# Rows of the normed activations at multiples of 256 bytes, and narrower stationary operands for one level of scores

## The chip, the cores and the metric

The kernel runs on one core of a Trainium2 chip. The metric is the device time of one execution in microseconds (us), the median of several runs. The profile shows one execution, instruction by instruction. TensorE appears there twice: PE for the products, PEld for the loads of the stationary operand. DVE is VectorE, ACT is ScalarE, POOL is GpSimd, SP issues the transfers from memory.

## The reference

One decoder layer over 16 meta tokens and 512 tokens of width 1024, in float32. Cut to what matters here:

```python
n = rmsnorm(h, norm_mix_g[l])                       # h: 16 meta tokens, then x
proj = n @ w_in[l]
zq, zf, zi, zog, zpool, zga, zgb = jnp.split(proj, SPLIT_POINTS, axis=-1)
...
o = hgrn2_chunked(...)                              # per head: decayed scores of q and k, times v
y_a = o * silu(zog);  y_b = pooled(zpool) @ pool_w * pool_scale
merged = sigmoid(zga) * (y_a @ w_branch_a[l]) + sigmoid(zgb) * (y_b @ w_branch_b[l])
h = h + merged @ w_out[l]
n2 = rmsnorm(h, norm_ffn_g[l])
h = h + (jax.nn.silu(n2 @ w_ffn_gate[l]) * (n2 @ w_ffn_up[l])) @ w_ffn_down[l]
return rmsnorm(h, norm_final_g)[:, N_META:]
```

## The kernel before

**Products in three terms.** Each large product is made in the type float32r from operands that are split into a high and a low part: high by high, low by high and high by low are added in one accumulator (`mm3`, lines 154 to 156). The weights stream from memory in blocks of 128 x 1024 (`wr`); ACT casts the high part (`wh`, line 130) and DVE subtracts for the low part (`wl`, line 137). In `product` a block of weights is the stationary operand, 128 columns at a time, and the transposed activations are the moving operand, 512 columns at a time, or in two pieces of 256 and 272 where the 16 meta tokens are needed too (`METAS`). In `token_major` (the output product `po` and the down product `pd`, lines 763 to 765) it is the other way round: the activations are stationary and 512 columns of weights move.

**The activations that move.** The first norm, transposed, lies in `nTh` and `nTl`: 128 partitions, 8 rows of `TT` = 528 elements each, one row for each 128 of the width (`k` in the code). A row is 528 x 4 = 2112 bytes, which is 8 times 256 and 64 more. So the rows begin at 0, 64, 128 and 192 bytes past a multiple of 256, and the same again for rows 4 to 7. They feed `pj_f`, `pj_v`, `pj_p` (pieces of 256 and 272) and `pj_q`, `pj_gb`, `pj_og`, `pj_ga` (512). The second norm lies in `n2h` and `n2l` with the same shape, in the same memory, though only 512 of the 528 columns are used; it feeds `pj_fg` and `pj_fu`, the gate and up products of the FFN. All other moving operands (`yah`, `ybh`, and the weights themselves in `po` and `pd`) have rows of 2048 or 1024 bytes and begin at multiples of 1024.

**Scores by levels.** The recurrence (`hgrn`, for four groups of two heads) computes its scores by levels of h = 1, 2, 4, ... 64. A level's products go into one bank `psc`; ACT copies the result into `scT`. Levels 16, 32 and 64 are made at line 523: for each 128-token block, keys of h tokens are stationary (h columns) and queries of the next h tokens move. These are float32 products, which the trace shows as two passes each. Level 64 has 8 products per group, 64 stationary by 64 moving columns.

**The order.** The program is written as generators that are woven together: after each step of `hgrn` some 6 to 9 steps of products for other branches follow (`weave`). A scheduler orders each engine's instructions from that.

Of the kernel before, what the change touches and what calls it, by code (L numbers as in the profile page):

```python
# [8 lines left out]
F32 = mybir.dt.float32  # L9
F32R = mybir.dt.float32r  # L10
# [5 lines left out]
P = 128  # L16
D = 1024
T = 512
NM = 16
TT = T + NM  # L20
KT = D // P
NH = 8
NG = 4
# [13 lines left out]
def hybrid_layer(ctx: ExitStack, tc: tile.TileContext, x, meta_tokens, norm_mix_g, w_in, lb_raw,  # L37
                 hgrn_norm_g, pool_w, pool_scale, w_branch_a, w_branch_b, w_out, norm_ffn_g,
                 w_ffn_gate, w_ffn_up, w_ffn_down, norm_final_g, out):
    nc = tc.nc  # L40
    cst = ctx.enter_context(tc.tile_pool(name="cst", bufs=1))
    wp = ctx.enter_context(tc.tile_pool(name="wp", bufs=3))
    big = ctx.enter_context(tc.tile_pool(name="big", bufs=1))
# [12 lines left out]
    def t5(name, cols=T):  # L56
        return sm.tile([P, TT], F32, tag="t5", name=name, bufs=8)[:, 0:cols]

    def bank(pool, name):
        return pool.tile([P, 512], F32, tag=pool.name, name=name)  # L60
# [134 lines left out]
        add_rows(w_ffn_down, DFF, half * 512, 512, 2)  # L195


    nTh = big.tile([P, KT, TT], F32R, tag="bigA", name="nTh")
    nTl = big.tile([P, KT, TT], F32R, tag="bigB", name="nTl")

    def squares(src, rows, name):
        sq = g4t(f"sq_{name}")
# [49 lines left out]
    nc.sync.dma_start(pw, pool_w[0].rearrange("g c d -> c g d"))  # L252


    par = cst.tile([P, 29], F32, name="par")
    lmx = cst.tile([P, 8], F32, name="lmx")
    le = cst.tile([P, 16], F32, name="le")
    lb = cst.tile([P, 8], F32, name="lb")
# [4 lines left out]
    def load_parameters():  # L263
        pps = bank(psm, "pps")
        nc.tensor.transpose(pps[:, 0:29], prow[0:29, :], ident[0:29, 0:29])
        nc.vector.tensor_copy(par, pps[:, 0:29])

    def parameters():
        nc.vector.tensor_tensor(lmx, par[:, 0:8], par[:, 8:16], ALU.max)
# [7 lines left out]

    NT = lambda k: (nTh[:, k, :], nTl[:, k, :])  # L280

    def pair(hs, ls):
        def f(k):
# [4 lines left out]
    def product(name, mov, nk, done, cuts=((0, T),)):  # L288

        pss = [[bank(psm, f"pj_{name}{j}{i}")[:, 0:b - a] for i, (a, b) in enumerate(cuts)] for j in range(2)]  # L290
        for k0 in range(0, nk, 4):
            wh, wl = W.get()
            for j in range(2):
                js = slice(j * P, (j + 1) * P)
                for k in range(4):
                    mh, ml = mov(k0 + k)
                    for ps, (a, b) in zip(pss[j], cuts):
                        mm3(ps, wh[:, k, js], wl[:, k, js], mh[:, a:b], ml[:, a:b],
                            k0 + k == 0, k0 + k == nk - 1)
                    yield  # L300
                if k0 + 4 == nk:
                    done(j, pss[j])

    CUT = 256
    METAS = ((0, CUT), (CUT, TT))

# [4 lines left out]
    def load_group(g, first=False):  # L311
# [7 lines left out]
        def f_done(hh, ps):  # L319
# [4 lines left out]
            nc.scalar.activation(fv[:, CUT:T], p1[:, 0:T - CUT], AF.Sigmoid)  # L324
            nc.scalar.activation(Fm[:, hh, :], p1[:, T - CUT:TT - CUT], AF.Sigmoid)
            for t, o in ((fv, kk[:, hh * T:(hh + 1) * T]), (Fm[:, hh, :], km[:, hh, :])):
# [7 lines left out]
        else:  # L334
            yield from product(f"f{g}", NT, KT, f_done, METAS)

        vT = []

        def v_done(hh, ps):
            t = t5(f"vT{g}{hh}", TT)  # L340
            nc.scalar.copy(out=t[:, 0:CUT], in_=ps[0])
            nc.scalar.copy(out=t[:, CUT:TT], in_=ps[1])
            vT.append(t)

        yield from product(f"v{g}", NT, KT, v_done, METAS)

# [4 lines left out]

        for i, _ in enumerate(product(f"q{g}", NT, KT, q_done)):
            yield
# [14 lines left out]
    def first_product(done):  # L368
# [13 lines left out]
        def part(i, b, passes=range(3)):  # L382
            a, e = METAS[i]
            h, l = W.parts[b]
            for p in passes:
                for j in range(2):
                    js = slice(j * P, (j + 1) * P)
                    for k in range(4):
                        mh, ml = NT(4 * b + k)
                        nc.tensor.matmul(pss[j][i], (h, l, h)[p][:, k, js], (mh, mh, ml)[p][:, a:e],  # L390
                                         start=b == 0 and p == 0 and k == 0, stop=b == 1 and p == 2 and k == 3)
# [31 lines left out]
        part(0, 1, (2,))  # L423
        mt = g4t("mt")[:, 0:KT * NM].rearrange("p (k t) -> p k t", t=NM)
        tm = bank(psh, "tp_m").rearrange("p (k t) -> p k t", t=NM)[:, 0:KT, :]
# [41 lines left out]
    def hgrn(g):  # L467

        F, kk, qq, Fm, km, vt, vm = grp[g]
        scT, Q, tt = g4t(f"scT{g}"), g4t(f"Q{g}"), g4t(f"tt{g}")  # L470
# [35 lines left out]
        for h in (1, 2, 4, 8, 16, 32, 64):  # L506
            ps = bank(psh, f"psc{g}_{h}")
            if h == 1:
                for c in range(4):
                    nc.tensor.matmul(ps[32 * c:32 * c + 32, 0:P], ones, E.rearrange(  # L510
                        "p (i w b) -> p i w b", i=8, w=4)[:, :, c, :], start=True, stop=True)
            elif h <= 8:
                n = 32 if h == 2 else 16
                for i, c in wins:
                    o = (4 * i + c) * 32
                    mv = M2[:, 4 * i + c, :] if h == 2 else halves(Q[:, o:o + 32], h)[1]
                    nc.tensor.matmul(ps[32 * c:32 * c + 32, i * n:(i + 1) * n], kk[:, o:o + 32], mv,
                                     start=True, stop=True)
            else:
                for i in range(8):  # L520
                    for b in range(0, P, 2 * h):
                        o = i * P + b
                        nc.tensor.matmul(ps[b:b + h, i * h:(i + 1) * h], kk[:, o:o + h],
                                         Q[:, o + h:o + 2 * h], start=True, stop=True)
            if h == 4:

                pk = bank(psh, f"pkm{g}")
                for hh in range(2):
                    nc.tensor.transpose(pk[:NM, hh * P:(hh + 1) * P], km[:, hh, :], ident)
                kmT = sm.tile([NM, 2 * P], F32, tag="kmT", name=f"kmT{g}", bufs=1)  # L530
                nc.vector.tensor_copy(kmT, pk[:NM, 0:2 * P])
            if h == 16:
                pS = bank(psh, f"pS{g}")
                for hh in range(2):
                    hs = slice(hh * P, (hh + 1) * P)
                    nc.tensor.matmul(pS[:, hs], kmT[:, hs], vm[:, hs], start=True, stop=True)
                S = sm.tile([P, 2 * P], F32, tag="S", name=f"S{g}_0", bufs=5)
                nc.vector.tensor_copy(S, pS[:, 0:2 * P])
                Ss = [S]
            widen(tot[h], h, kk, Q)  # L540
            if h > 1:
                totals(tot[h], h, 1024 // h, tot[2 * h])
            if h == 1:
                nc.scalar.copy(out=M2[:, :, 16:32].rearrange("p w (b h) -> p w b h", h=2),
                               in_=halves(Q, 2)[1].rearrange("p (w b) h -> p w b h", b=8))
                nc.vector.tensor_tensor(dS[:, :, 0:32:2], ps[:, 0:P].rearrange("p (i b) -> p i b", i=8),
                                        mask[:, 0, :].unsqueeze(1).to_broadcast([P, 8, 16]), ALU.mult)
            elif h <= 8:
                v = ps[:, 0:256 if h == 2 else P].rearrange("p (i c) -> p i c", i=8)
                if h == 2:  # L550
                    nc.vector.tensor_tensor(dS[:, :, 1:32:2], v[:, :, 0:16],
                                            mask[:, 1, :].unsqueeze(1).to_broadcast([P, 8, 16]), ALU.mult)
                    v = v[:, :, 16:32]
                nc.vector.copy_predicated(
                    dS.rearrange("p i (b two h) -> p i b two h", two=2, h=h)[:, :, :, 1, :],
                    masked({2: 2, 4: 3, 8: 4}[h], h), v.rearrange("p i (b h) -> p i b h", h=h))
                if h == 8:
                    for c in range(4):
                        nc.scalar.copy(out=sc4[32 * c:32 * c + 32, :, 32 * c:32 * c + 32],
                                       in_=dS[32 * c:32 * c + 32])  # L560
            else:
                for b in range(0, P, 2 * h):
                    nc.scalar.copy(out=sc4[b:b + h, :, b + h:b + 2 * h],
                                   in_=ps[b:b + h, 0:8 * h].rearrange("p (i c) -> p i c", i=8))
            yield
# [31 lines left out]
        for cp in range(2):  # L597
            po = bank(psh, f"po{g}_{cp}")
            for c2 in range(2):
                c = 2 * cp + c2  # L600
                for hh in range(2):
# [4 lines left out]
                                     start=False, stop=True)  # L606
# [21 lines left out]
    def pool_sums(i):  # L628
# [19 lines left out]

        yield from product(f"p{i}", NT, KT, p_done, METAS)

# [23 lines left out]
    def branch_b(j):  # L674
        sgs, done = gates(f"b{j}")
        yield from product(f"gb{j}", NT, KT, done)
        mB[j] = g4t(f"mB{j}")
# [111 lines left out]
        h1.append(big.tile([P, D], F32, tag=f"tok{c}", name=f"h1_{c}"))  # L789
    gfb = g4t("gfb")  # L790
    nc.sync.dma_start(gfb, norm_ffn_g[0].partition_broadcast(P))
    n2h = big.tile([P, KT, TT], F32R, tag="bigA", name="n2h")
    n2l = big.tile([P, KT, TT], F32R, tag="bigB", name="n2l")
    n2 = [None] * NC

    def ev_out(half, c, ps):
# [114 lines left out]
```

## Time and profile before

| | us |
|---|---|
| median of 3 runs | 863.45 (862.47 to 864.07) |
| the profiled execution, its own time | 862.53 |
| its span, first to last instruction | 860.8 |
| PE busy | 848.8 |
| PEld busy | 717.9 |
| DVE busy | 380.6 |
| ACT busy | 280.1 |

The duration of one matmul in the profile covers its way through the array, so durations of neighbours overlap. What a product costs the kernel is the distance between starts: from the start of the first product of a stretch to the start of the first one after it, divided by their number. Durations in ns (`mean ns`) serve to compare like with like.

### The profile page before, as it was taken

The numbers are of one execution on the slowest core, as the hardware profiler recorded it, in microseconds if no ns is written. First come the engines' busy times: TensorE is split into PE (matmuls) and PEld (weight loads), VectorE is DVE, ScalarE is ACT, GpSimd is POOL, SyncE is SP. The second block draws the span as 40 slices with busy tenths as digits, with TensorE's granted clock in tenths as the row PEclk, the third lists the DMA queues.
The fourth block names the chain that finished last, engine by engine and source line by source line (L and its number), as shares of the span: only waits on it lengthen the run. The fifth ranks groups of instructions, "written<-read, shape, count | busy, mean of one in ns | idle before, by whom it ended". The sixth has DMA issues, their size and how long they took to land.

```text
span 860.8 us, 12910 instructions
## 1 busy us (share of the span) xinstructions
PE 848.8 (99%) x5561; PEld 717.9 (83%) x5561; DVE 380.6 (44%) x566; ACT 280.1 (33%) x428; POOL 33.8 (4%) x69
## 2 busy tenths in 40 slices
PE   7999999999999999999999999999999999999996
PEld 7989987898898788888888888888888888888885
DVE  4657537435644656443333733333333333323214
ACT  5434333334333344333222532222222222213111
POOL 4200010001001001000000100000000000000001
PEclk9999999999999999999999999999999999999999
DMA  7322122222221231333263233333333332323312
GB/s 260 98 89 86 54 71 75 93 80 67 81 78 49 79 94 51 97 99 97 98 220 98 60 112 86 90 95 99 97 98 98 97 92 84 120 97 99 98 50 97
DMA packets 68595, 81.39 MB, mean 95 GB/s; under 512 B 2573, under 2 KB 58410, under 8 KB 68538
## 3 DMA queue, kind: packets, MB, share of 16 engines
q1 hardware_dynamic: 68538, 80.57, 30.0%
q8 instruction: 43, 0.70, 0.3%
q14 instruction: 14, 0.11, 0.0%
HBM read 78.46 MB, written 2.10 MB: 94 GB/s over the span
## 4 chain that ended last, share of the span: by engine, by line
PE 96%; DVE 1%; DMA 1%; POOL 1%; ACT 0%; issue 0%; SPq 0%; POOLq 0%; ACTq 0%
PE pj_fu L155 5%; PE pj_fu L156 5%; PE pj_fu L154 5%; PE pj_fg L156 5%; PE pj_fg L155 5%; PE pj_fg L154 5%; PE pd L763 4%; PE pd L765 4%; PE pd L764 4%; PE pj_gb L154 2%; PE pj_v L154 2%; PE pj_v L156 2%; PE pj_v L155 2%; PE pj_gb L155 2%; PE pj_ga L155 2%; PE pj_q L156 2%
## 5 line engine op out<-in xcount | busy, mean ns | idle before, releaser
L137 DVE TENSOR_TENSOR wl<-wr,wh 128x1024 fp32r<-128x1024 f32 x137 | 167.8, 1225 | 335.7 <-ACT wh L130 332.1
L130 ACT CAST wh<-wr 128x1024 fp32r<-128x1024 f32 x138 | 145.1, 1051 | 330.9 <-issue 75.1
L156 PE MATMUL pj_fg<-n2h,wl 128*128 128x512 f32 (+1 forms) x192 | 72.1, 376 | 0.2 <-DVE wl L137 0.2
L155 PE MATMUL pj_fg<-n2l,wh 128*128 128x512 f32 (+1 forms) x192 | 72.2, 376 | 0.0
L154 PE MATMUL pj_fg<-n2h,wh 128*128 128x512 f32 (+1 forms) x192 | 71.8, 375 | 0.2 <-ACT n2h L227 0.2
L155 PE MATMUL pj_fu<-n2l,wh 128*128 128x512 f32 x176 | 69.6, 395 | 0.0
L156 PE MATMUL pj_fu<-n2h,wl 128*128 128x512 f32 x176 | 69.2, 393 | 0.0
L154 PE MATMUL pj_fu<-n2h,wh 128*128 128x512 f32 x176 | 68.9, 393 | 0.0
L764 PE MATMUL pd<-wl,hidh 128*128 128x512 f32 (+1 forms) x176 | 66.2, 376 | 0.0
L763 PE MATMUL pd<-wh,hidh 128*128 128x512 f32 (+1 forms) x176 | 66.2, 376 | 0.0
L765 PE MATMUL pd<-wh,hidl 128*128 128x512 f32 (+1 forms) x176 | 66.1, 376 | 0.0
L154 PEld LDWEIGHTS pj_fg<-n2h,wh 128*128 128x128 f32 x192 | 36.0, 188 | 7.7 <-ACT n2h L227 0.5
L156 PEld LDWEIGHTS pj_fg<-n2h,wl 128*128 128x128 f32 x192 | 36.1, 188 | 7.4 <-DVE wl L137 0.6
L155 PEld LDWEIGHTS pj_fg<-n2l,wh 128*128 128x128 f32 x192 | 36.0, 188 | 7.2 <-DVE n2l L230 0.2
L154 PEld LDWEIGHTS pj_fu<-n2h,wh 128*128 128x128 f32 x176 | 33.0, 188 | 7.8
L155 PEld LDWEIGHTS pj_fu<-n2l,wh 128*128 128x128 f32 x176 | 33.0, 188 | 7.7
L156 PEld LDWEIGHTS pj_fu<-n2h,wl 128*128 128x128 f32 x176 | 33.1, 188 | 7.4
L764 PEld LDWEIGHTS pd<-wl,hidh 128*128 128x128 f32 x176 | 33.1, 188 | 6.1
L765 PEld LDWEIGHTS pd<-wh,hidl 128*128 128x128 f32 x176 | 33.1, 188 | 6.1
L763 PEld LDWEIGHTS pd<-wh,hidh 128*128 128x128 f32 x176 | 33.1, 188 | 6.1
L154 PE MATMUL pj_v<-nTh,wh 128*128 128x256 f32 (+1 forms) x128 | 36.9, 288 | 0.0
L156 PE MATMUL pj_v<-nTh,wl 128*128 128x256 f32 (+1 forms) x128 | 36.4, 285 | 0.0
(234 smaller groups left out, 1698.2 us busy)
## 6 DMA issues: line engine op xcount, KB each, us to landing
wr<-in_w_in_dram SPq DMA_DIRECT2D x52, 512.0 KB, 3.5
wr<-in_w_ffn_gate_dram SPq DMA_DIRECT2D x22, 512.0 KB, 3.7
wr<-in_w_ffn_up_dram SPq DMA_DIRECT2D x22, 512.0 KB, 3.7
wr<-in_w_ffn_down_dram SPq DMA_DIRECT2D x22, 512.0 KB, 3.5
wr<-in_w_branch_a_dram SPq DMA_DIRECT2D x8, 512.0 KB, 3.3
wr<-in_w_out_dram SPq DMA_DIRECT2D x8, 512.0 KB, 3.5
x<-in_x_dram SPq DMA_DIRECT2D x4, 512.0 KB, 5.3
wr<-in_w_branch_b_dram SPq DMA_DIRECT2D x4, 512.0 KB, 3.4
```

What stands on the lines that cost most here:

```text
L130: nc.scalar.copy(out=h, in_=self.raw[i])
L137: eng.tensor_sub(l, self.raw[i], f32(self.parts[i][0]))
L154: nc.tensor.matmul(ps, sh, mh, start=first, stop=False)
L155: nc.tensor.matmul(ps, sh, ml, start=False, stop=False)
L156: nc.tensor.matmul(ps, sl, mh, start=False, stop=last)
L763: nc.tensor.matmul(pt, sh[:, cs], w[0][:, k, a:e], start=first, stop=False)
L764: nc.tensor.matmul(pt, sh[:, cs], w[1][:, k, a:e], start=False, stop=False)
L765: nc.tensor.matmul(pt, sl[:, cs], w[0][:, k, a:e], start=False, stop=last)
```

## The change

Four edits. The rows of `nTh` and `nTl` become `TR` = 576 elements, 2304 bytes, 9 times 256; `NT` hands out the first 528 of them. The rows of `n2h` and `n2l` become 512 elements, 2048 bytes. The small constant tile `par` gets 93 columns in place of 29, of which 29 are used. And at levels over 32 the keys are taken 32 at a time: level 64 has 16 products of 32 stationary columns in place of 8 of 64.

```diff
+TR = 576
...
-    nTh = big.tile([P, KT, TT], F32R, tag="bigA", name="nTh")
-    nTl = big.tile([P, KT, TT], F32R, tag="bigB", name="nTl")
+    nTh = big.tile([P, KT, TR], F32R, tag="bigA", name="nTh")
+    nTl = big.tile([P, KT, TR], F32R, tag="bigB", name="nTl")
...
-    par = cst.tile([P, 29], F32, name="par")
+    par = cst.tile([P, 93], F32, name="par")
...
-        nc.vector.tensor_copy(par, pps[:, 0:29])
+        nc.vector.tensor_copy(par[:, 0:29], pps[:, 0:29])
...
-    NT = lambda k: (nTh[:, k, :], nTl[:, k, :])
+    NT = lambda k: (nTh[:, k, 0:TT], nTl[:, k, 0:TT])
...
             else:
+                m = min(h, 32)
                 for i in range(8):
                     for b in range(0, P, 2 * h):
                         o = i * P + b
-                        nc.tensor.matmul(ps[b:b + h, i * h:(i + 1) * h], kk[:, o:o + h],
-                                         Q[:, o + h:o + 2 * h], start=True, stop=True)
+                        for a in range(0, h, m):
+                            nc.tensor.matmul(ps[b + a:b + a + m, i * h:(i + 1) * h], kk[:, o + a:o + a + m],
+                                             Q[:, o + h:o + 2 * h], start=True, stop=True)
...
-    n2h = big.tile([P, KT, TT], F32R, tag="bigA", name="n2h")
-    n2l = big.tile([P, KT, TT], F32R, tag="bigB", name="n2l")
+    n2h = big.tile([P, KT, T], F32R, tag="bigA", name="n2h")
+    n2l = big.tile([P, KT, T], F32R, tag="bigB", name="n2l")
```

Where the tiles lie follows from the build. Before, the weight blocks begin at byte 20480 of a partition, `nTh` at 57344, `nTl` at 74240, the activations of the branches and of the FFN's hidden layer at 107520 and at steps of 4096 from there. After, the 256 bytes more of `par` move the weights to 20736 and `nTh` to 57600; `nTl` begins at 76032 and the activations at 110848. So both kernels have their large tiles at multiples of 256, and after the change nearly all of them at odd multiples: 20736 is 81 times 256, 57600 is 225 times, 110848 is 433 times. What differs in the remainder by 256 is only the rows inside `nTh`, `nTl`, `n2h` and `n2l`.

The order of the instructions hardly moves. On PE, in each of the four groups, the products of level 64 stand at the same place as before (`psc_64` is the bank of the level, `k` the keys, `Q` the queries; the figures are stationary by moving columns). Group 1, before:

```order
L155 MATMUL pj_f_1978<-nTl,wh_1979 128x272
L156 MATMUL pj_f_1978<-nTh,wl_1981 128x272
L523 MATMUL psc_64_2098<-Q_1561,k_1070 64x64 x8
L154 MATMUL pj_f_1977<-nTh,wh_1979 128x256
L155 MATMUL pj_f_1977<-nTl,wh_1979 128x256
```

and after:

```order
L156 MATMUL pj_f_1986<-nTl,wh_1987 128x272
L157 MATMUL pj_f_1986<-nTh,wl_1989 128x272
L526 MATMUL psc_64_2106<-Q_1569,k_1070 32x64 x16
L155 MATMUL pj_f_1985<-nTh,wh_1987 128x256
L156 MATMUL pj_f_1985<-nTl,wh_1987 128x256
```

Only the level itself differs, 16 products in place of 8. On DVE the order changes at one place, around level 64 of the last group (`ya` and `yal` belong to the branch that is woven in, `wl` is a low part of the weights, the two rows that write `Q` and `k` widen the decays after level 64). Before:

```order
L692 TENSOR_TENSOR ya_3548<-ya_3548,oT_1526 128x512
L463 TENSOR_TENSOR Q_3158<-Q_3158,tt_3159 128x8x64
L465 TENSOR_TENSOR k_2667<-k_2667,tt_3159 128x8x64
L694 TENSOR_TENSOR yal_3410<-ya_3548,yah_3409 128x512
L137 TENSOR_TENSOR wl_3614<-wr_3492,wh_3612 128x1024
```

and after:

```order
L695 TENSOR_TENSOR ya_3572<-ya_3572,oT_1534 128x512
L138 TENSOR_TENSOR wl_3646<-wr_3516,wh_3644 128x1024
L697 TENSOR_TENSOR yal_3434<-ya_3572,yah_3433 128x512
L464 TENSOR_TENSOR Q_3182<-Q_3182,tt_3183 128x8x64
L466 TENSOR_TENSOR k_2683<-k_2683,tt_3183 128x8x64
```

There `wl` and `yal` now stand ahead of the two widenings; on ACT, accordingly, the copy of level 64 into `scT` stands behind a cast of `yah` and no longer ahead of it.

## Rows read from the trace of the kernel before

**Rows 1.** The page: busy us, share of the span and count of each engine.
```profile
PE 848.8 (99%) x5561; PEld 717.9 (83%) x5561; DVE 380.6 (44%) x566; ACT 280.1 (33%) x428; POOL 33.8 (4%) x69
```

**Rows 2.** The longest of PE's six waits: for whom, us in total, times, longest.
```profile
PE tp_x L222 <- DVE n_x L211: 2.4, 2, 2.0
```

**Rows 3.** Busy us by stretch: length, engines, granted clock, DMA share, GB/s.
```profile
125.00:220.00 95.00, 95.00 (x829) 80.70 (x828) 50.84 (x89) 33.87 (x58) 3.31 (x5) 1.00 0.25 78
...
620.00:720.00 100.00, 100.00 (x433) 81.10 (x432) 34.93 (x38) 29.44 (x37) 0.00 (x0) 1.00 0.32 95
```

**Rows 4.** Timeline of PE, last gate, branch, output product: start, duration, form.
```profile
417.93 0.39 PE L154 MATMUL pj_ga<-nTh,wh 128*128 128x512 f32 x1
...
429.07 0.39 PE L154 MATMUL pj_a<-yah,wh 128*128 128x512 f32 x1
...
439.97 0.39 PE L763 MATMUL po<-wh,mh 128*128 128x512 f32 x1
...
475.33 1.13 PE L222 MATMUL tp_h<-ident,n_h 128*128 128x128 f32 x8
```

**Rows 5.** Timeline of PE: start of the second gate product, and of the down product.
```profile
510.85 0.39 PE L154 MATMUL pj_fg<-n2h,wh 128*128 128x512 f32 x1
...
733.25 0.39 PE L763 MATMUL pd<-wh,hidh 128*128 128x512 f32 x1
```

**Rows 6.** Single matmuls (busy us, mean ns), starting at 566.452, 567.142 and 560.892 us.
```profile
L154 PE MATMUL pj_fu<-n2h,wh 128*128 128x512 f32 x1 | 0.4, 388 | 0.0
...
L154 PE MATMUL pj_fu<-n2h,wh 128*128 128x512 f32 x1 | 0.4, 396 | 0.0
...
L154 PE MATMUL pj_fg<-n2h,wh 128*128 128x512 f32 x1 | 0.4, 388 | 0.0
```

**Rows 7.** Timeline of PE: pieces of 256 and 272 columns, at three places.
```profile
29.38 0.28 PE L154 MATMUL pj_v<-nTh,wh 128*128 128x256 f32 x1
...
41.03 0.39 PE L154 MATMUL pj_q<-nTh,wh 128*128 128x512 f32 x1
...
494.75 0.31 PE L155 MATMUL pj_fg<-n2l,wh 128*128 128x256 f32 x1
...
500.18 0.39 PE L155 MATMUL pj_fu<-n2l,wh 128*128 128x512 f32 x1
...
851.82 0.28 PE L763 MATMUL pd_h<-wh,hidh 128*128 128x256 f32 x1
...
853.86 0.28 PE L765 MATMUL pd_h<-wh,hidl 128*128 128x256 f32 x1
```

**Rows 8.** Timeline of PE around levels 1, 32 and 64 of the scores.
```profile
58.48 0.43 PE L510 MATMUL psc<-E,ones 128*32 128x128 f32 x8
58.84 0.38 PE L154 MATMUL pj_p<-nTh,wh 128*128 128x256 f32 x1
...
89.19 0.70 PE L523 MATMUL psc<-Q,k 128*32 128x32 f32 x32
89.82 0.39 PE L154 MATMUL pj_f<-nTh,wh 128*128 128x256 f32 x1
...
95.11 1.15 PE L523 MATMUL psc<-Q,k 128*64 128x64 f32 x16
96.18 0.39 PE L154 MATMUL pj_f<-nTh,wh 128*128 128x256 f32 x1
```

**Rows 9.** Timeline of DVE and PE after level 64 of the last group.
```profile
312.12 0.69 DVE L692 TENSOR_TENSOR ya<-ya,oT 128x512 f32<-128x512 f32 x1
...
313.67 0.69 DVE L465 TENSOR_TENSOR k<-k,tt 128x512 f32<-128x512 f32 x1
314.27 0.68 DVE L694 TENSOR_TENSOR yal<-ya,yah 128x512 fp32r<-128x512 f32 x1
314.87 1.22 DVE L137 TENSOR_TENSOR wl<-wr,wh 128x1024 fp32r<-128x1024 f32 x1
...
317.22 0.27 PE L572 MATMUL pkt<-ident,k 128*128 128x128 f32 x1
```

## The prediction

> **What bounds the kernel now.** I read the page first: PE is busy 848.8 of 860.8 us, more than twice as long as any other engine [rows 1]. Then PE's waits: six entries, the longest 2.4 us in total, for the first norm [rows 2]. Then two stretches, one where the recurrence is woven in and one of the FFN: PE is busy throughout, at full granted clock, while DVE is busy for 53% and 35%, ACT for 36% and 29%, and transfers take a quarter to a third of the queues [rows 3]. So between the first norm and the last matmul, time is what PE's instructions take one behind the other. Distances between starts then decide, and there like products differ. The last `pj_ga` takes 429.07 - 417.93 = 11.14 us for 48 products of 512 columns, 232.1 ns each; the `pj_a` behind it, with the same shapes and the same kind of weights in the same loop, 10.90 us or 227.1 ns; `po` 35.36 us for 156, 226.7 ns [rows 4]. The FFN's gate and up products from 510.85 to 733.25 us are 20 times 48: 222.40 us / 960 = 231.7 ns [rows 5]. Slow are those that stream `nTh`, `nTl`, `n2h`, `n2l` with rows of 2112 bytes; fast are those that stream operands at multiples of 1024.
>
> Is it where a row begins? The pattern inside one product says so. The first matmul streams row 0, at a multiple of 512: 388 ns. Three later, row 1, 64 bytes past a multiple of 256: 396 ns. Row 4 begins at an odd multiple of 256, and takes 388 again, here in the gate product before [rows 6]. The remainder by 256 sets the duration, and an odd multiple is as good as an even one.
>
> **The change part by part.**
>
> *Products of 512 columns.* 16 products on `nTh` and `nTl` (four each of `pj_q`, `pj_gb`, `pj_og`, `pj_ga`) and 21 on `n2h` and `n2l` (ten gate, eleven up), 48 matmuls each: 1776. All their rows now begin at multiples of 256. I take 231.7 - 226.7 = 5.0 ns each: 8.9 us less. The bounds are 231.7 - 227.1 = 4.6 ns (8.2 us) and, from `pj_ga`, 232.1 - 226.7 = 5.4 ns (9.6 us) [rows 4, 5]. I take 226.7 and not 227.1 because products of this kind will follow one another, as in `po`. All of it lies on the path: no wait appears on PE there, and the engines that feed it are busy for about half of their time or less [rows 2, 3].
>
> By the Trainium skill, "SBUF — State Buffer", Specifications (TRN2), the line of this memory is 16 bytes, and only crossing to a new one costs. All rows begin at multiples of 64 before the change too, so by that rule this term would be zero and the sum 862.7. The rows disagree: 8 ns lie between row 0 and row 1, both at the start of such a line.
>
> *Products of 256 and 272 columns.* Here the regular row is not the faster one. `pj_v` takes 41.03 - 29.38 = 11.65 us for 96 matmuls, half of either width: 121.4 ns. At the end, 256 columns from multiples of 1024 take (853.86 - 851.82) / 17 = 120.0 ns [rows 7]. 512 columns at 226.7 and 256 at 120.0 make 106.7 ns for 256 columns and a fixed 13.3; 272 would take 126.7, and the mean of both widths 123.3, which is 1.9 ns more than now. That holds for 384 of `pj_v`, 288 of `pj_f`, 192 of `pj_p` and 96 at the start of the FFN, 960 in all: 1.8 us more. The bounds are 0 and 2.0 ns each (1.9 us): the start of the FFN takes 500.18 - 494.75 = 5.43 us for 46 matmuls of 256 columns from `n2h` and `n2l`, 118.0 ns against 120.0 [rows 7]. The first 96 of `pj_f` run where PE waits for DVE [rows 2]; I cost them at nothing.
>
> *Level 64.* Now 8 products of 64 by 64 take 96.18 - 95.11 = 1.07 us, 16 passes of 67 ns; level 32, 16 products of 32 by 32, takes 0.63 us, 32 passes of 20 ns. A pass of half the stationary columns costs under a third. Afterwards there are 32 passes with 32 stationary and 64 moving columns, which the trace does not show. From below, level 32: 0.63 us. From above, with the same stationary width and twice the moving one, level 1: 0.36 us for 8 passes of 128 columns, 45 ns, or 1.44 us for 32 [rows 8]. I take 0.67 us, near level 32, since level 1 spreads its entry and exit over 8 passes and not 32. That is 0.4 us less, and with four groups 1.6 us less; the ends are 1.8 us less and 1.5 us more. No engine hides it: PE goes from a projection into the level and back without a gap.
>
> The Trainium skill speaks against this edit: "TensorEngine Tiling (Array Packing)", Instruction Overhead, gives each matmul about 60 cycles however little it streams. As an estimate by that page, 64 passes more at 60 cycles of 2.4 GHz would add 1.6 us and the sum would be 857.0. Level 32 disagrees: its passes take 20 ns with entry and exit, less than 25.
>
> *DVE's order in the last group.* The widening of `k` moves behind `wl` and `yal`. It would end at 312.12 + 0.69 + 1.22 + 0.68 + two widenings of 0.69 = 316.09 us, and the transposes that read it start at 317.22, some 0.5 us earlier after the change [rows 9]. About 0.6 us of slack stay: nothing. If the cover is gone, PE waits some tenths of a us, once; I allow 0.5. The copy into `scT` on ACT moves by one cast and is read only by the output products of the group, several steps later: nothing.
>
> *The rest.* The unused columns of `par`, and the longer steps between rows when `nTh` is written, change no count and no size. Weights are needed 2% sooner in the FFN; SP's transfers take 32% of the queues there [rows 3].
>
> **Sum.** 862.53 - 8.9 + 1.8 - 1.6 = 853.8 us against the profiled execution. That one lies 0.9 us under the median of the runs, 863.45, so I forecast **854.7 us** for the median.
>
> **The rivals.**
>
> *Where a row begins is not the cause* (0.09). The slow operands also differ as large tiles with eight rows, where the fast ones are pairs of rows in tiles of their own. Then only level 64 remains: 862.53 - 1.6 + 0.9 = 861.8. Against it: rows 0 and 4 are fast inside the same tile [rows 6].
>
> *Odd multiples of 256 are bad, and the change moves everything onto them* (0.05): the slower side. `pj_a`, `pj_b`, `po` and `pd` move 942 operands of 512 columns that were at multiples of 1024 and now begin at odd multiples of 256. If only multiples of 512 are cheap, one row in eight was cheap before, and a bad one costs 5.0 x 8/7 = 5.7 ns: 942 x 5.7 = 5.4 us more, the FFN's products lose their one cheap row (126 x 5.7 = 0.7 us), while the first norm's 768 go from seven bad rows in eight to four (1.6 us less). With level 64 that is 862.53 + 5.4 + 0.7 - 1.6 - 1.6 + 0.9 = 866.3. It decides on row 4: it would have to read 396 ns, and reads 388 [rows 6].
>
> *Narrow products pay per pass* (0.04): 32 passes at the 67 ns of today make 2.14 us, 1.07 us more in each group: 854.7 + 1.6 + 4.3 = 860.6. Against it: level 32 [rows 8].
>
> **How the numbers follow.** The forecast has 0.82. Its own ends: 862.53 - 9.6 - 1.8 + 0.9 = 852.0, and 862.53 - 8.2 + 1.9 + 1.5 + 0.5 + 0.9 = 859.1. The runs before spread by 0.9 us to either side, so I set 851.5 to 860.0; outside remain the rivals and a little of the forecast's own, not over 2 in 10. A measurement of this kernel tells about 0.2%, 1.7 us, from no change. Faster by more: the forecast, the third rival and a little of the first, 0.87. Within it: most of the first rival, 0.08. Slower: the second, 0.05.
>
> **What would show it.** Right: the 20 gate and up products in a row take 217.6 us and not 222.4, with 388 to 389 ns on every row; `pj_ga` as long as `pj_a`, 10.9; `pj_v`'s first 96 matmuls 11.84 us and not 11.65; level 64 as 32 passes in some 0.67 us; no new wait on PE at `pkt`. Wrong: `po` or `pd` over 227 ns (odd multiples), gate products still at 231.7 (not the row), or a level 64 of over 1.07 us.

## The result, and the profile after

The changed kernel takes **854.79 us** (median of 4 runs, 854.33 to 854.87) against 863.68 us (4 runs, 862.47 to 864.07) before: a ratio of 0.9898, 95% interval 0.9881 to 0.9915. The forecast was 854.7. The execution profiled took 854.87 us, 7.66 less than the one profiled before. The medians lie further apart, 8.89 us; executions of one kernel differ by up to 2 us with their mean granted clock (the kernel before, on another chip, from 861.90 us at 0.998 to 863.87 at 0.994), and the two profiled ones are alike in it, 0.997 and 0.996.

The page after, busy time by engine; it answers to [rows 1]:

```profile
span 853.2 us, 13039 instructions
...
PE 841.2 (99%) x5625; PEld 718.5 (84%) x5625; DVE 380.4 (45%) x566; ACT 280.2 (33%) x428; POOL 33.8 (4%) x69
```

PE has 64 matmuls more and 7.6 us less to do; DVE and ACT stand where they stood. PE's waits after, which answer to [rows 2] (for whom, us in total, times, longest):

```profile
PE tp_x L223 <- DVE n_x L212: 2.3, 2, 2.0
...
PE pot L623 <- DVE on L615: 0.2, 1, 0.2
```

The second of these is new, and worth 0.2 us. None has appeared in one of the large products. The gain can therefore only have come out of what PE's own instructions take, one behind the other. Timeline of PE after, the places of [rows 4] and [rows 5], then of [rows 7]:

```profile
415.48 0.39 PE L155 MATMUL pj_ga<-nTh,wh 128*128 128x512 f32 x1
...
426.36 0.39 PE L155 MATMUL pj_a<-yah,wh 128*128 128x512 f32 x1
...
437.24 0.39 PE L766 MATMUL po<-wh,mh 128*128 128x512 f32 x1
...
508.07 0.39 PE L155 MATMUL pj_fg<-n2h,wh 128*128 128x512 f32 x1
...
725.67 0.39 PE L766 MATMUL pd<-wh,hidh 128*128 128x512 f32 x1
```

```profile
29.49 0.28 PE L155 MATMUL pj_v<-nTh,wh 128*128 128x256 f32 x1
...
41.22 0.40 PE L155 MATMUL pj_q<-nTh,wh 128*128 128x512 f32 x1
...
844.22 0.28 PE L766 MATMUL pd_h<-wh,hidh 128*128 128x256 f32 x1
...
846.26 0.28 PE L768 MATMUL pd_h<-wh,hidl 128*128 128x256 f32 x1
```

The last `pj_ga` takes 426.36 - 415.48 = 10.88 us (11.14 before), and the `pj_a` behind it the same 10.88: 226.7 ns for each of 48. The FFN's 20 gate and up products take 725.67 - 508.07 = 217.60 us and not 222.40, 226.7 ns each and not 231.7. The first 96 of `pj_v` take 11.73 us (11.65 before, 11.84 forecast); `pd_h` stays at 2.04 us for 17. Duration of the up products' first term, shortest, median and longest in ns, before:

```profile
L154 PE MATMUL pj_fu<-n2h,wh x176: 387/394/399, 494.3 to 732.6; 128*128 128x512 f32 x176
```

and after, where the rows have become alike:

```profile
L155 PE MATMUL pj_fu<-n2h,wh x176: 389/389/397, 491.6 to 725.0; 128*128 128x512 f32 x176
```

Levels 32 and 64 of the first group after, as in [rows 8], each with the product behind it:

```profile
89.34 0.70 PE L526 MATMUL psc<-Q,k 128*32 128x32 f32 x32
89.96 0.39 PE L155 MATMUL pj_f<-nTh,wh 128*128 128x256 f32 x1
...
95.29 1.09 PE L526 MATMUL psc<-Q,k 128*32 128x64 f32 x32
96.31 0.39 PE L155 MATMUL pj_f<-nTh,wh 128*128 128x256 f32 x1
```

Level 64 takes 96.31 - 95.29 = 1.02 us, 32 passes where there were 16, and 1.07 before. That is far from the 0.67 forecast. The last group's widening of `k` and the transposes that read it, DVE and PE, as in [rows 9]:

```profile
314.10 0.69 DVE L466 TENSOR_TENSOR k<-k,tt 128x512 f32<-128x512 f32 x1
...
316.05 0.82 PE L575 MATMUL pkt<-ident,k 128*128 128x128 f32 x6
```

The widening ends at 314.79 us, 1.26 us before the transposes start, and PE does not wait for it. Before, it ended at 314.36 and they started at 317.22, 2.86 us later [rows 9].

**Where the 7.66 us come from.** I added the distances between starts for each product over the whole trace, before and after. All wide ones: `pj_fu` 122.33 to 119.72 us, `pj_fg` 123.48 to 121.23 (its 96 narrow matmuls included), `pj_ga` 44.52 to 43.52, `pj_og` 45.60 to 44.81, `pj_gb` 46.57 to 45.82, `pj_q` 46.30 to 45.65, together 8.05 less. Narrow ones: `pj_v` 47.35 to 47.61, `pj_f` 50.57 to 50.87, `pj_p` 24.05 to 24.22, together 0.73 more. All levels of the scores: 18.85 to 18.62, 0.23 less. `pj_a` and `pj_b`: 0.12 less. The sum is -7.67; all the rest of PE's work takes 0.05 more, and the span went from 860.78 to 853.16 us, -7.62. The forecast's terms add up to -8.7, so they promised 1 us too much. Against the profiled execution the forecast was 853.8, and that execution took 854.87; why the median was met all the same is said below, under the total.

### The profile page after: what moved, and what is told of

It is laid out like the page before. It is cut to its first block, busy times and chain, and to the rows that moved or that the text cites. A ratio compares the mean times of both kernels' runs of the same rounds, so it can differ in the third digit from the quotient of the medians.

```text
span 853.2 us, 13039 instructions
## 1 busy us (share of the span) xinstructions
PE 841.2 (99%) x5625; PEld 718.5 (84%) x5625; DVE 380.4 (45%) x566; ACT 280.2 (33%) x428; POOL 33.8 (4%) x69
## 4 chain that ended last, share of the span: by engine, by line
PE 96%; DVE 1%; DMA 1%; POOL 1%; ACT 1%; issue 0%; SPq 0%; POOLq 0%; ACTq 0%
PE pj_fg L157 5%; PE pj_fg L155 5%; PE pj_fu L155 5%; PE pj_fu L157 5%; PE pj_fg L156 5%; PE pj_fu L156 5%; PE pd L767 4%; PE pd L768 4%; PE pd L766 4%; PE pj_v L155 2%; PE pj_gb L155 2%; PE pj_v L156 2%; PE pj_v L157 2%; PE pj_q L155 2%; PE pj_q L157 2%; PE pj_q L156 2%
## 5 line engine op out<-in xcount | busy, mean ns | idle before, releaser
L156 PE MATMUL pj_v<-nTl,wh 128*128 128x256 f32 (+1 forms) x128 | 36.5, 285 | 0.0
```

Of the source, the lines that this page charges most:

```text
L156: nc.tensor.matmul(ps, sh, ml, start=False, stop=False)
```

## The experiments

**1. The edits apart.** The first kernel has only the rows of `nTh`, `nTl`, `n2h`, `n2l` changed, the second only level 64, the third only the 64 unused columns of `par`.

```diff
 e1_rows:    TR = 576, NT(... 0:TT), n2h and n2l of T columns; par and level 64 as before
 e2_level64: for a in range(0, h, m): ... kk[:, o + a:o + a + m] ...; the rest as before
 e3_par:     par = cst.tile([P, 93], F32, name="par"); the rest as before
```

> Only the rows: nTh and nTl with 576 elements, n2h and n2l with 512; par and level 64 as in the kernel before. If the rows carry the gain: 864 - 8.9 + 0.7 = about 855.2 us, within 0.4 of the changed kernel, products of 512 columns at 226.7 ns each, pj_v's first 96 matmuls 11.7 to 11.8 us. If level 64 is worth the 1.6 us of the prediction, this one must be 1.6 us slower than the changed kernel, 856.4. If the shift of all tiles by 256 bytes is what helps, it stays at 863.7.

> Only level 64 with 32 stationary columns; rows as before. By the trace of the changed kernel (32 passes, 1.02 us against 1.07): 0.2 us less than before, 863.5, not to be told from no change. By the prediction's price (0.67 us per group): 862.1. The products of 512 columns on nTh and n2h stay at 231.7 to 232.1 ns.

> Only par with 93 columns: every tile from the weights on moves by 256 bytes, to odd multiples of 256; rows of 2112 bytes stay. If the remainder by 256 alone counts: as before, 863.7, and pj_a, po and pd at 226.7 to 227.1 ns. If odd multiples of 256 are dear (the slower rival): pj_a, pj_b, po and pd at 232 ns and some 5 us more, 869.

Measured: 855.15 us with the rows alone (ratio 0.9918, 0.9903 to 0.9932), 862.83 with level 64 alone (1.0002, 0.9993 to 1.0011), 862.48 with `par` alone (0.9997, 0.9987 to 1.0006); before, on this chip, 862.52. The rows carry the gain; the other two edits can't be told from no change. Timeline of PE of the second kernel, level 64 of the first group:

```profile
95.21 1.09 PE L525 MATMUL psc<-Q,k 128*32 128x64 f32 x32
96.22 0.38 PE L154 MATMUL pj_f<-nTh,wh 128*128 128x256 f32 x1
```

1.01 us again, without the rows. And the third kernel, last `pj_ga`, `pj_a` and first `po`; the weights and the activations of `pj_a` and `po` now begin at odd multiples of 256:

```profile
417.46 0.39 PE L154 MATMUL pj_ga<-nTh,wh 128*128 128x512 f32 x1
...
428.60 0.39 PE L154 MATMUL pj_a<-yah,wh 128*128 128x512 f32 x1
...
439.50 0.39 PE L763 MATMUL po<-wh,mh 128*128 128x512 f32 x1
```

`pj_a` stays at 439.50 - 428.60 = 10.90 us. An odd multiple of 256 costs nothing: the rival that had the kernel slower at 866.3 is out. Nor does it matter that one operand lies at an odd multiple and the other at an even one: in the first kernel the weights stay at even multiples and the rows alternate, and the `pj_ga` products take 226.7 ns there.

**2. Level 64: what paces a pass.** The changed kernel with 32 moving columns in place of 64 at this level, by which half of the level's scores are left out.

```diff
-nc.tensor.matmul(ps[..., i * h:(i + 1) * h], kk[:, o + a:o + a + m], Q[:, o + h:o + 2 * h], ...)
+nc.tensor.matmul(ps[..., i * h:i * h + m], kk[:, o + a:o + a + m], Q[:, o + h:o + h + m], ...)
```

> The changed kernel, with level 64's products moving 32 columns and not 64: half of that level's scores are left out (and not copied), the number of passes stays at 32 per group. If the moving columns set the pace of a pass: the level takes 0.63 us as level 32 does, 16 ns between passes, 4 x 0.39 = 1.6 us less in all. If the number of passes or the loads of the stationary operand set it: 1.02 us as in the changed kernel, no change in all.

Measured: 853.88 us (0.9886, 0.9858 to 0.9915). Its level 64 on PE:

```profile
95.38 0.70 PE L526 MATMUL psc<-Q,k 128*32 128x32 f32 x32
96.01 0.38 PE L155 MATMUL pj_f<-nTh,wh 128*128 128x256 f32 x1
```

0.63 us for 32 passes, as level 32. All levels together take 17.07 us over the trace and not 18.62, and the profiled execution is 1.50 us shorter than that of the changed kernel (853.37 against 854.87), as expected; two runs are few for the median. Between starts of passes lie on average 16.2 ns with 32 moving columns and 28.0 with 64, at 32 stationary columns in both. So at this width the moving columns set the pace. Halving the stationary columns halved a pass as well (1.07 us / 16 = 67 ns before, 1.02 / 32 = 32 after, with entry and exit), but it doubled the number of passes. Inside the level, passes started 58 ns apart before (median); after, they start in pairs, 7 ns and then 49 ns apart, so a pair takes nearly what one pass took.

**3. Is it the start of the moving operand?** The prediction said that the remainder by 256 of the row that streams sets the duration. Here the rows are as in the changed kernel, but the weights `wr`, `wh`, `wl` alone are moved to 64 past a multiple of 256, then to 128 past; a tile `gap` behind them brings the activations back to multiples of 256. In the projections weights are stationary; in `po` and `pd` they move.

```diff
 e4_w64:  par of 45 columns (weights + 64 bytes against the kernel before),  gap = big.tile([P, 48], F32, ...)
 e5_w128: par of 61 columns (weights + 128 bytes), gap = big.tile([P, 32], F32, ...)
```

> The changed kernel, with the weight blocks (wr, wh, wl) alone moved to 64 bytes past a multiple of 256; an unused gap ahead of nTh, filled once by POOL, keeps all activations at multiples of 256. If the start of the moving operand sets the price: only po and pd, where weights move, get slower, from 226.7 to about 232.4 ns (the rate of row 1 in the kernel before): 654 x 5.7 = 3.7 us more, 858.5; pj_ga, pj_a, pj_fg, pj_fu stay at 226.7. If it was the change of the remainder from row to row, or rows inside one large tile: no change, 854.8. If the stationary operand's start counts as well: all products slower, 1776 + 942 matmuls by up to 5.7 ns, 15 us more, 870.

> As the run with the weights at 64 bytes past a multiple of 256, but at 128 past. If 256 is the step that counts: po and pd at about 232.5 ns again (row 2 of the kernel before), 3.7 us more than the changed kernel, 858.5. If multiples of 128 are as good: 226.7 ns, 854.8.

Measured: 866.37 us (1.0049, 1.0033 to 1.0066) and 870.09 (1.0074, 1.0045 to 1.0103), both slower than the kernel before. Weights 64 past, last `pj_ga`, `pj_a`, first `po`:

```profile
418.88 0.39 PE L155 MATMUL pj_ga<-nTh,wh 128*128 128x512 f32 x1
...
430.08 0.39 PE L155 MATMUL pj_a<-yah,wh 128*128 128x512 f32 x1
...
441.28 0.40 PE L768 MATMUL po<-wh,mh 128*128 128x512 f32 x1
```

Both projections take 11.20 us, 233.3 ns each, though what they stream begins at multiples of 256. The stationary operand's start counts too. The same places with the weights 128 past:

```profile
420.47 0.39 PE L155 MATMUL pj_ga<-nTh,wh 128*128 128x512 f32 x1
...
431.62 0.39 PE L155 MATMUL pj_a<-yah,wh 128*128 128x512 f32 x1
...
442.78 0.40 PE L768 MATMUL po<-wh,mh 128*128 128x512 f32 x1
```

Here they take 232.4 ns each. For this kernel 858.5 or 854.8 us was expected, and neither came, since both figures left the projections at 226.7. The step of the prediction as it stood is refuted, though its total held.

**4. Each operand's own remainder, or the difference?** Two readings are left: every operand has to be at a multiple of 256, or stationary and moving operand have to agree. In the first kernel all large tiles, weights and activations, lie 64 past a multiple of 256; in the second the activations alone.

```diff
 e8_all64: par of 109 columns (weights, nTh + 320 bytes against the kernel before)
 e9_act64: par of 93 columns as in the change, gap = big.tile([P, 16], F32, ...) ahead of the activations
```

> The changed kernel with every large tile, weights and activations alike, 64 bytes past a multiple of 256 (par with 109 columns). In the run with the weights alone moved, products whose moving operand lay at multiples of 256 got slower too (233.3 ns). If what counts is the difference of the two remainders, stationary against moving: it is 0 again here, 226.7 ns everywhere and 854.8 us. If each operand's own remainder counts: products of 512 columns at 233 ns or more, 866 to 870 us.

> The changed kernel with the weights at multiples of 256 and all activations at 64 past one (an unused gap ahead of nTh). Rows of nTh and n2h now all have the same remainder, 64. If the remainder of the moving operand counts: pj_ga, pj_a, pj_fg, pj_fu at 232 to 233.3 ns, as in the run with the weights moved; about 1968 + 96 matmuls by 6 ns, 867 us. If only a change of the remainder from one row to the next hurts the moving operand: 226.7 ns there, 854.8 us.

Measured: 856.13 us (0.9924, 0.9905 to 0.9944) and 863.18 (0.9999, 0.9989 to 1.0009). All 64 past:

```profile
416.73 0.39 PE L155 MATMUL pj_ga<-nTh,wh 128*128 128x512 f32 x1
...
427.61 0.39 PE L155 MATMUL pj_a<-yah,wh 128*128 128x512 f32 x1
...
438.49 0.39 PE L766 MATMUL po<-wh,mh 128*128 128x512 f32 x1
```

10.88 us for either product, 226.7 ns, as fast as at multiples of 256. Activations alone 64 past:

```profile
418.11 0.39 PE L155 MATMUL pj_ga<-nTh,wh 128*128 128x512 f32 x1
...
429.09 0.39 PE L155 MATMUL pj_a<-yah,wh 128*128 128x512 f32 x1
...
440.09 0.39 PE L768 MATMUL po<-wh,mh 128*128 128x512 f32 x1
...
852.35 0.28 PE L768 MATMUL pd_h<-wh,hidh 128*128 128x256 f32 x1
...
854.28 0.28 PE L770 MATMUL pd_h<-wh,hidl 128*128 128x256 f32 x1
```

10.98 and 11.00 us. So for a product of 512 columns to run at 226.7 ns the two operands have to agree in the remainder by 256, and it may be 64 as well as 0. Other equal remainders were not tried.

The 1.3 us by which the first kernel lies above the changed one are not in these products. They arise before `pj_v` starts, at 30.75 us and not at 29.49: the first `pj_f` is longer (`pj_f` 51.63 us in all and not 50.87), and PE's wait for `n_x` is 2.9 us and not 2.3. The granted clock differs there. From 11.60 to 18.30 us (length, PE busy, granted clock, DMA share, GB/s) in the first kernel, in the changed one, and in the changed one run again for experiment 6:

```profile
11.60:18.30 6.70, 6.39 (x29) 0.50 0.91 268
...
11.60:18.30 6.70, 6.38 (x39) 0.75 0.83 272
...
11.60:18.30 6.70, 6.47 (x54) 1.00 0.88 271
```

The clock was at its lower level, 1.2 GHz, for all of this stretch, for half of it, and for none of it; before it fell, PE had made its first transposes, with waits for the norm between them. `pj_v` starts at 30.75, 29.49 and 28.82 us. The last two are one kernel, so a difference of this kind needs no change of where the tiles lie.

**5. Does half the step do?** Rows of 544 elements, 2176 bytes, so that rows begin at 0 and 128 past a multiple of 256 in turn.

```diff
-TR = 576
+TR = 544
 (n2h and n2l with rows of TR too)
```

> The changed kernel with rows of 544 elements (2176 bytes, 8.5 times 256) in nTh, nTl, n2h and n2l: rows begin at 0 and 128 past a multiple of 256 in turn. If only multiples of 256 are cheap: products of 512 columns between 229 and 232.5 ns, 4 to 9 us more than the changed kernel. If multiples of 128 do: 226.7 ns and 854.8 us.

Measured: 863.83 us against 863.72 before (1.0006, 0.9994 to 1.0017): nothing is gained, though half of the rows agree with the weights. Last `pj_ga`, `pj_a`, first `po`:

```profile
419.97 0.39 PE L155 MATMUL pj_ga<-nTh,wh 128*128 128x512 f32 x1
...
431.09 0.39 PE L155 MATMUL pj_a<-yah,wh 128*128 128x512 f32 x1
...
442.02 0.39 PE L766 MATMUL po<-wh,mh 128*128 128x512 f32 x1
```

`pj_ga` takes 11.12 us, 231.7 ns; the up products of the FFN take 232.2. If each matmul paid for its own row, it would be the mean of 226.7 and 232.4 (experiment 3, 128 past), 229.6. The rows that agree are not the cheap ones either: in the ten up products whose 48 matmuls follow without a break, the distance from start to start is 233.5 ns on average for rows 0, 2, 4 and 6, which agree, and 231.0 for the others. So what a matmul costs depends on the matmuls around it too; by what rule was not found.

**6. A better cut.** 272 columns take longer from rows that agree (126.3 ns against 124.8 before), 256 do not; the second piece began at column 256, 1024 bytes into the row, and so agreed as well. Cut at column 272 instead, the second piece begins 1088 bytes in, 64 past. This was run twice, the second time beside the changed kernel.

```diff
+    CUT2 = 272
+    METAS2 = ((0, CUT2), (CUT2, TT))
...
-        yield from product(f"v{g}", NT, KT, v_done, METAS)
+        yield from product(f"v{g}", NT, KT, v_done, METAS2)
 (pj_p and all but the first pj_f likewise)
```

> The changed kernel with the pieces of pj_v, pj_p and the later pj_f cut at column 272 and not 256: 272 columns first, then 256 that begin 64 bytes past a multiple of 256. In the run with the weights moved, narrow pieces were faster off the multiples (pd_h at 113.3 ns against 120.0). If that holds for a moving operand alone: pieces of 256 at 113 to 117 ns against 118.1, up to 432 x 4 = 1.7 us less, 853 to 854.5 us, the fastest of all. If they pay as the wide ones do: no change or some 1 us more.

> The changed kernel again, beside the next kernel on one chip, so that the two can be told apart. Expected 854.8 us, as before, between 854.3 and 855.3.

> The changed kernel with the products of 528 columns cut at 272 and 256 from column 272 on (pj_v, pj_p and the later part of pj_f). By the products' own rows (pj_v 47.61 to 47.27 us, pj_p 24.22 to 24.03) 0.5 to 0.6 us below the changed kernel of the same call: 854.2 where that is 854.8. A rival: the gain of the narrow products is lost in the waits behind them, and the two are within 0.2 us.

Measured, first time: 853.80 us (853.44 to 854.98; ratio 0.9896, 0.9879 to 0.9913), too wide to tell it from the changed kernel. Second time: 854.08 us (854.05 to 854.16; ratio to before 0.9896, 0.9880 to 0.9913), and the changed kernel beside it 854.74 (854.21 to 854.79; 0.9902, 0.9888 to 0.9917). No run of the one reaches into those of the other, so 0.66 us less, where 0.5 to 0.6 was expected; the ratios to before overlap, and four runs of each are few. Its first `pj_v`:

```profile
29.59 0.29 PE L155 MATMUL pj_v<-nTh,wh 128*128 128x272 f32 x1
...
41.22 0.39 PE L155 MATMUL pj_q<-nTh,wh 128*128 128x512 f32 x1
```

11.63 us where the changed kernel takes 11.73. Over the trace `pj_v` takes 47.27 us and not 47.61, `pj_p` 24.03 and not 24.22, and `pj_f` behind its first 96 matmuls 37.00 and not 37.24. In the first `pj_v` the pieces of 272, whose start did not change, fell from 126.4 to 125.1 ns, and those of 256 from 118.0 to 117.2. This is the fastest version here that computes everything.

## Why the prediction was right, and where it was not

- **What bounds.** Right. PE is busy for 99% of the span after as before, and the distances between starts in the products account for the whole difference (-7.67 us, where the span lost 7.62).
- **Products of 512 columns, forecast -8.9.** Right in place and nearly in size: 8.2 us, which is the 8.05 above and the 0.15 that the narrow matmuls of `pj_fg` took more. The FFN gave the 4.8 us that was forecast for its 20 products, at the 226.7 ns chosen. Short were `pj_q`, `pj_gb` and `pj_og`: 0.65, 0.75 and 0.79 us for 192 matmuls each, 3.4 to 4.1 ns and not 5.0. `pj_ga`, with hardly anything woven in, gave 1.00 us, 5.2 ns. The two traces tell where the rest went. The 109 matmuls of `pj_q` that follow at least four others of it, and are followed by one, fell from 232.0 to 227.1 ns; the other 83, next to what is woven in, went only from 21.01 to 20.90 us.
- **The reason given for it** was incomplete, and that is the step that failed. "The remainder by 256 sets the duration" was read from rows 0, 1 and 4 of one moving tile [rows 6], with all weights at multiples of 256. In those rows the moving operand's remainder and its difference from the stationary one are the same number, so the view could not tell them apart. Experiments 3 and 4 did. Besides, those three rows are all first terms. The matmul right behind the first of them, from 566.68 us, streams row 0 of `n2l`, which begins at a multiple of 512 too:

```profile
L155 PE MATMUL pj_fu<-n2l,wh 128*128 128x512 f32 x1 | 0.4, 398 | 0.0
```

398 ns, more than the 396 of row 1; 236 ns pass from its start to the next, and 226 from that of the first. So already in the trace before, a row's own start did not set what its matmul took; the mean over all of a product is what the change lowered. The forecast for these products held because the change leaves the weights at a multiple of 256. The line of 16 bytes in the Trainium skill, "SBUF — State Buffer", Specifications (TRN2), does not account for it: every start of these operands in all these kernels is at a multiple of 64, and the same matmul takes 226.7 to 233.3 ns.

- **Narrow pieces, forecast +1.8.** Mis-sized: 0.8 us for the 960 matmuls, 0.26 in `pj_v`, 0.20 in the later `pj_f`, 0.17 in `pj_p` and 0.15 at the start of the FFN (12.28 to 12.43 us). The fixed part of 13.3 ns was taken from `pd_h`, 120.0 ns for 256 columns, and carried over to the projections. There 256 columns stayed at 118.0 ns (first `pj_v`), and only those of 272 rose, from 124.8 to 126.3 (expected: 126.7). At the start of the FFN 256 columns did go from 118 to 120 ns (medians).
- **Level 64, forecast -1.6.** Mis-sized: 0.06 us per group, 0.23 in all. "Near level 32" was the wrong neighbour. Level 32 has both its stationary and its moving columns at half of level 64's, and I put its short pass down to the stationary ones. Halving those took a pass from 67 to 32 ns, which the doubled number of passes uses up. The step from there to level 32 is in the moving columns, as experiment 2 shows: 28.0 ns between starts at 64, 16.2 at 32. By the Trainium skill, "TensorEngine Tiling (Array Packing)", Instruction Overhead, some 60 cycles for each matmul would have made it 1.6 us dearer; no run shows that, and 16.2 ns on average between starts of passes is under 60 cycles of 2.4 GHz (25 ns).
- **DVE's order, forecast 0.** Right that it costs nothing. The slack fell from 2.86 us to 1.26, not to 0.6: the widenings did move behind `wl` and `yal`, but ended at 314.79 us and not at 316.09, and the transposes started 1.2 us earlier and not 0.5.
- **The rivals.** All fell: the rows alone give a ratio of 0.9918; odd multiples cost nothing (experiment 1); level 64 did not become dearer.
- **The total.** Level 64 gave 1.4 us too little, and the wide products 0.7; the narrow ones cost 1.0 less than forecast, and `pj_a` and `pj_b` gave 0.1 that was not forecast. So the sum of 853.8 us missed the profiled execution's 854.87 by 1.1. The median was met to 0.1 us because 0.9 us had been added for the distance between the profiled execution and the median before; in the changed kernel's runs there is no such distance (854.87 profiled, 854.79 median). These two errors cancelled, and that is luck.

## What to carry to other kernels

Read the distance between starts of like products in different places; 5 ns of 230 on a thousand matmuls is 5 us where PE is the bound. If they differ, compare where stationary and moving operand begin: in this kernel products of 512 columns want the same remainder by 256 in every row, and padding rows to a multiple of 256 with all large tiles at one remainder gave 1%. When one row of a trace stands in for an operation that isn't there, ask which of its sizes differ from what is wanted: two at once can't be told apart.

## What was unexpected

- **What counts is whether the starts agree, not where one of them lies.** 512 moving columns, same kernel otherwise, means over whole products: equal remainders 226.7 ns, whether both 0 or both 64. Unequal ones, in the gate and up products with 128 stationary columns: moving operand 64 ahead 228.9, 128 apart 232.4, stationary 64 ahead 233.3. In `pd`, where the weights move, it is the same by direction: 228.9 with the weights 64 ahead, 233.3 with the activations (first 282 matmuls). `po` is an exception, 233.3 for its first 156 either way. The means hide a pattern: with the activations 64 ahead, the three terms of an up product take 225.8, 229.2 and 231.7 ns on every row, though all three have the same remainders. That stationary operands are loaded while others stream (PEld is busy for 84% of the span and PE for 99%), and that the two reads meet in the memory, would fit; it was not tested, a load takes 188 ns (median, first term of `pj_fu`) before as after, and why direction and `po` differ stays open.
- **In `pd_h`, with 256 columns, it is the other way round.** It takes 2.04 us for 17 with equal remainders, 120.0 ns each, and 854.28 - 852.35 = 1.93 us with activations 64 past, 113.5. In the first `pj_v`, where pieces of 256 and 272 alternate, the pieces of 256 hardly tell: 118.0 ns equal, 117.2 with the weights 64 past, 118.4 with the activations. Where a product can be cut in many ways, unequal starts are worth a try for the narrow pieces, as experiment 6 shows in small. Why is open.
- **Alternating remainders are as dear as constant unequal ones**: 231.7 to 232.2 ns where every second row agrees, 232.4 where none does (experiments 5 and 3).
